# A two-block transformer kernel on one core: token norm folded into the activation before the expert matmuls, GpSimd sums as adding DMAs, gate products on VectorE, a third gelu buffer

## The chip, the cores and the metric

One Trainium2 (trn2) chip, one core. The metric is the device time of one execution in microseconds (us). The kernel before took 2830.65 us in the median of 3 runs (2825.29 to 2832.58).

## The reference, cut to what matters

256 tokens of width 2048 go through two blocks. The change lies in the second half of the first one, a layer of 16384 experts (128 x 128), of which every token uses 128.

```
hn = rms_norm(h, ffn_norm_gain)                      # per token
q = (hn @ w_query).reshape(T, 8, 2, 128)
scores = einsum('thpc,hpnc->thpn', q, sub_keys)
vals, idx = top_k(scores, 16)                        # then the best 16 of 16 x 16 sums
experts, gates = ...                                 # 128 experts and softmax gates per token
u = expert_down[experts]                             # rows of 16384 x 2048
hdn = gelu(einsum('ted,td->te', u, hn))
h = h + einsum('te,ted->td', gates * hdn, expert_up[experts])
```

## The kernel before, in words

Everything is float32. A weight is streamed in units of 128 x 2048 (1 MB) through three raw buffers by SyncE's DMA queue (line 69). Each unit is cut in two halves; of each half ScalarE writes the rounded part `hi` (line 74) and VectorE the rest `lo` (line 75), into five half buffers `whl`. `fm` (lines 100 to 102) then multiplies a unit with the activation `act`, itself a pair hi and lo, by 3 x 16 matmuls of 256 columns: 48 matmuls a unit.

The expert layer (`phase_peer`) computes the dense product for all 16384 experts and picks afterwards:

- **Query**: 16 units of `w_pq`; ScalarE, VectorE and GpSimd find the top 16 (top-k) beside it.
- **Down stage**: 128 units of `expert_down`, in 32 groups of four. Per unit, VectorE multiplies the sums in PSUM with the token's norm factor (`Rb`, line 1007, into `z`), and ScalarE applies gelu into `ghs` (line 968), a buffer of 128 x 4 x 256 for one group; there are two. `act` holds the activation without the norm, since the factor is the same for all features of a token.
- **Place steps**, beside the down stage: 64 steps of four tokens build the dense gate matrix. VectorE makes two one-hot tiles `oe`, `oa` (lines 690, 691); GpSimd (line 698) and ScalarE (line 700) multiply `oe` with the two parts of the gate into `ob`; TensorE places them (line 710, 4 matmuls); ScalarE (717) and VectorE (722) add the parts into `gst`, a buffer for 16 tokens, of which there are two. Every fourth step `used` stores `gst` to `g_d` in HBM from ScalarE's queue (738), and GpSimd adds it to `fsum` (740, 742), which VectorE sums into `F` after 8 of them (744).
- **Before the last place step** the gates are not there yet, so finished gelu groups go to HBM (`gh_d`): they are "late". Afterwards `catch_up`, once per unit, lets GpSimd load a late group into `ght` (892; two buffers), multiply it with the gates `gt` (882; loaded from `g_d`, 877, 1 MB per two groups) and store it to `hm_d` (885). New groups are multiplied in `ghs` (882) and stored from there (885), by the same GpSimd queue.
- **List steps**, beside the catch-up: the list of experts that any token uses (lines 826, 828, 836, 837, matmuls 845).
- **Up stage**: rows of `expert_up` and of `hm_d` are gathered by that list.

The side work is spread over the units by a credit: each unit gives `DV` = 2.6 us (`pump_by`), each step costs what its `step(us, ...)` says, 2.3 for a place step and 2.2 for a list step. Before the fifth unit from the end `drain` runs what is left. Engine queues are in program order.

```
def hidden(j, a, gh, z):
    nc.scalar.activation(gh[:, a, :], z, AF.Gelu_apprx_tanh)
...
    x = pp.tile([128, 4, 256], F32, name="ght", tag="ght%d" % (j % 2))
    nc.gpsimd.dma_start(x.rearrange("p a t -> p (a t)"), gh_d[j])
```

Of the kernel before, what the change touches and what calls it, by code (L numbers as in the profile page):

```python
# [9 lines left out]
F32 = mybir.dt.float32  # L10
# [6 lines left out]
OP = mybir.AluOpType  # L17
# [13 lines left out]
KT = K0 + K1 + KB  # L31
JS = 31
FAR = float(1 << 20)
DV = 2.6
LN2_50 = 34.657359027997264


# [119 lines left out]
def after(k, n, f):  # L157

    k.due.setdefault(k.tick + n, []).append(f)
# [12 lines left out]
def pump_by(k, us):  # L172

    k.credit = min(k.credit + us, 2 * us)
    if not k.bg:
        pump(k)
    while k.bg and k.credit > 0:
        k.credit -= getattr(k.bg[0], "us", 1.5)
        pump(k)


def step(us, f):
    f.us = us
    return f
# [378 lines left out]
def phase_peer(k, A):  # L563
# [5 lines left out]
    with ExitStack() as ctx:  # L569
# [111 lines left out]
        def bc(x):  # L681
            return x[:, :, None].to_broadcast([128, 4, 128])
# [11 lines left out]
        def gates_at(q):  # L694
            ts = slice(4 * q, 4 * q + 4)
            b = pw.tile([128, 4, 2, 128], F32R, name="ob", tag="ob")
            e = hot[q][1]
            nc.gpsimd.tensor_mul(b[:, :, 1, :], e, bc(slot["g"][:, 1, ts].bitcast(F32)))  # L698
            for j in range(4):
                nc.scalar.mul(b[:, j, 0, :], e[:, j, :], slot["g"][:, 0, 4 * q + j:4 * q + j + 1].bitcast(F32))  # L700
            hot[q][1] = b
# [33 lines left out]

        def used(g, x):

            nc.scalar.dma_start(g_d[g], x.rearrange("p i t -> p (i t)"))
            if g % 8 == 0:
                nc.gpsimd.tensor_copy(fsum, x)  # L740
            else:
                nc.gpsimd.tensor_add(fsum, fsum, x)
            if g % 8 == 7:
                nc.vector.tensor_reduce(F[g // 8], fsum, axis=AX.X, op=OP.add)


        L = {}

        def lists_flags():
            stri = pp.tile([128, 128], F32, name="stri")  # L750
            nc.vector.tensor_sub(stri, k.tri, k.ident)
            f = pw.tile([128, 2, 128], F32, name="f01", tag="oh")
            for t in range(2):
                nc.vector.tensor_scalar(f[:, t, :], F[t], 0.0, None, op0=OP.is_gt)
            nc.vector.memset(f[:, :, 4 * JS:4 * JS + 4], 0.0)
            cat = L["cat"] = pw.tile([128, 3, 128], F32, name="cat", tag="oh")
            nc.vector.tensor_mul(cat[:, 2, :], f[:, 0, :], f[:, 1, :])
            for t in range(2):
                nc.vector.tensor_sub(cat[:, t, :], f[:, t, :], cat[:, 2, :])
            L["stri"] = stri  # L760
# [103 lines left out]
        def lists_end():  # L864
            t = pp.tile([128, 2, KT], F32, name="lv")
            nc.scalar.copy(t.rearrange("p e r -> p (e r)"), L["ps"][:, :2 * KT])
            nc.vector.scalar_tensor_tensor(t[:, 0, :], t[:, 1, :], 128.0, t[:, 0, :], op0=OP.mult, op1=OP.add)
            L["idx"] = indices(t[:, 0, :], KT, "l")
            L["ex"] = pp.tile([128, 128], F32, name="lex")
            nc.vector.tensor_scalar(L["ex"], iota, 128.0, pi, op0=OP.mult, op1=OP.add)  # L870


        Gs, late = {}, deque()
# [13 lines left out]
        def load_late(j):  # L887
            if j // 2 not in Gs:
                Gs.clear()
                Gs[j // 2] = load_g(j // 2, "gst%d" % (j // 2 % 2))  # L890
            x = pp.tile([128, 4, 256], F32, name="ght", tag="ght%d" % (j % 2))
            nc.gpsimd.dma_start(x.rearrange("p a t -> p (a t)"), gh_d[j])
            return x, Gs[j // 2]

        def rows(x, hi, lo, t):
            nc.scalar.copy(hi[:, t], x[:, t])
            nc.vector.tensor_sub(lo[:, t], x[:, t], hi[:, t].bitcast(F32))  # L897

        for g in range(16):
            w = st.next()  # L900
            acc = bank(k, "acc")[:, :256]
            if g == 0:
                fm(k, acc, w, k.act, part=(0, 12))
                drain(k)
                fm(k, acc, w, k.act, part=(12, 16))
                z0 = pw.tile([1, 256], F32, name="z0", tag="z", bufs=3)
                nc.gpsimd.memset(z0, 0.0)
                nc.gpsimd.dma_start(hm_d[0:1, :], z0)
            else:
                fm(k, acc, w, k.act)  # L910
            if g == 1:
                ms = k.p_sm.tile([128, 2], F32, name="ms", tag="ms")
                mean_eps(k, ms, k.ss, D)
                rsqrt(k, r, ms)
            if g == 4:
                row_bc(k, Rb, r)
            qT = pw.tile([128, 256], F32, name="qT", tag="qT")
            nc.scalar.copy(qT, acc)
            if g < 2:
                pump(k)  # L920
            else:
                pump_by(k, 3.2)
            k.bg.appendleft(step(0.0, lambda g=g, qT=qT: scores(g, qT)))
            if g % 2:
                k.bg.extend(topk_steps(g // 2))
        state = {}

        def prepare():

            def lag():  # L930
                return step(DV, lambda: None)
            yield step(0.7, last[0])
            for _ in range(3):
                yield step(0.3, lambda: None)
            yield step(2.0, gates)
            yield lag()
            yield step(0.6, to_slots)
            yield lag()
            yield step(1.4, lambda: ones_at(0))
            yield step(1.4, lambda: (ones_at(1), gates_at(0)))  # L940
            for q in range(65):
                yield step(2.3, lambda q=q: place_steps(q))

            def placed():
                state["placed"] = True
            yield step(0.0, placed)
            yield lag()
            yield step(2.0, lists_flags)
            yield lag()
            yield step(0.2, lists_count)  # L950
            yield lag()
            yield step(0.2, lists_sum)
            yield lag()
            yield step(2.5, lists_over)
# [9 lines left out]

        pend = deque()

        def hidden(j, a, gh, z):
            nc.scalar.activation(gh[:, a, :], z, AF.Gelu_apprx_tanh)
            if a < 3:
                return  # L970
            if "placed" not in state:
                nc.scalar.dma_start(gh_d[j], gh.rearrange("p a t -> p (a t)"))
                late.append(j)
                return
            if state.get("g") != j // 2:
                state["g"], state["gt"] = j // 2, load_g(j // 2, "gtd")
            times(gh, state["gt"], j)
            if j == JS:
                hst = state["hst"] = pp.tile([128, 2, 4, 256], F32R, name="hst", tag="gst%d" % (JS // 2 % 2))
                split(k, hst[:, 0], hst[:, 1], gh)  # L980
            else:
                store(j, gh)
# [16 lines left out]
        for i in range(NE):  # L999
            j, a = ORDER[i // 4], i % 4  # L1000
            w = st.next()
            acc = bank(k, "acc")[:, :256]
            fm(k, acc, w, k.act)
            if a == 0:
                gh = pw.tile([128, 4, 256], F32, name="ghs", tag="ghs")
            z = pw.tile([128, 256], F32, name="z", tag="z", bufs=3)
            nc.vector.tensor_mul(z, acc, Rb)
            if i:
                hidden(*prev)
            prev = (j, a, gh, z)  # L1010
# [35 lines left out]
        def overflow():  # L1046
            d = L["d"]
            nc.vector.tensor_scalar(d, d, -128.0 * KT, None, op0=OP.add)
            turns = nc.values_load(L["nx"][0:1, 1:2], min_val=0, max_val=NE)
            with k.tc.If(turns > 0), k.tc.For_i(0, turns, 1) as _:  # L1050
                ps = bank(k, "bg")
                for c in range(NE):
                    a = pw.tile([128, 128], F32, name="xa", tag="xa")
                    nc.vector.tensor_scalar(a, iota, d[:, c:c + 1], None, op0=OP.is_equal)
                    nc.tensor.matmul(ps[:, :1], a, L["ex"][:, c:c + 1], start=c == 0, stop=c == NE - 1)
# [643 lines left out]
```

## Time and profile before

| | |
|---|---|
| median of 3 runs | 2830.65 us |
| the profiled execution | 2830.46 us, span of its instructions 2828.7 us |
| busy share of the span | TensorE 94%, weight loads 86%, VectorE 67%, ScalarE 50%, GpSimd 30% |
| mean granted TensorE clock | 0.973 of full speed |
| moved by DMA | 580.26 MB, 205 GB/s |

The page gives shares over the whole span. Cut by stage they differ widely, so the rows below are windows. A row of a timeline reads: start us, duration us, engine, line, operation, written tile <- read tiles, shapes, and in brackets the idle time before it with what ended it. A group row ends with busy us, mean ns | idle us before, and what ended it.

### The profile page before, as it was taken

To read this page: it belongs to the slowest core of one execution; us is meant where nothing else is said; L and a number is where in the kernel's file an instruction comes from. 1 tells how busy PE (TensorE), PEld (TensorE's weight loads), DVE (VectorE), ACT (ScalarE), POOL (GpSimd) and SP (SyncE) were. 2 spreads that over 40 slices of the span, in tenths; PEclk is the share of its full clock that TensorE was granted. 3 is DMA by queue.
4 is the path that set the end of the run, shared out by engine and by line. 5 is a ranking of instruction groups with operands and counts; after the bars stand their busy time and mean duration, and the time that the engine had idled before them with its cause. 6 is when DMAs were issued, how large, how long until landed. Compare 5 with 4: busy or idle time off the path is not lost. (4 is left out here: it accounts for less than half of the span.)

```text
span 2828.7 us, 45188 instructions
## 1 busy us (share of the span) xinstructions
PE 2654.1 (94%) x18008; PEld 2423.3 (86%) x18008; DVE 1894.3 (67%) x2736; ACT 1409.3 (50%) x2298; POOL 848.6 (30%) x829
## 2 busy tenths in 40 slices
PE   8999999999988988966599999999999999999998
PEld 8977778999988988966597888887899999999886
DVE  5544556999899899755465666666567766555555
ACT  5344455444655566422244555556564444444453
POOL 0001110222244344344514565554145441000001
PEclk9999999999999999978799999999999999999999
DMA  7534435556655655777766888885543445555553
GB/s 281 170 128 136 160 122 180 178 201 217 216 195 194 215 198 213 286 251 275 234 203 235 296 290 295 288 300 189 206 165 135 150 150 185 192 186 187 185 188 134
DMA packets 92391, 580.26 MB, mean 205 GB/s; under 512 B 11216, under 2 KB 11344, under 8 KB 31120
## 3 DMA queue, kind: packets, MB, share of 16 engines
q1 hardware_dynamic: 53696, 381.05, 38.6%
q0 software_dynamic: 31712, 165.63, 16.8%
q10 hardware_dynamic: 6768, 30.65, 2.7%
q8 instruction: 143, 2.34, 0.3%
q14 instruction: 72, 0.59, 0.1%
HBM read 531.14 MB, written 46.14 MB: 204 GB/s over the span
## 5 line engine op out<-in xcount | busy, mean ns | idle before, releaser
L75 DVE TENSOR_TENSOR whl<-raw,whl 128x1024 fp32r<-128x1024 f32 (+2 forms) x917 | 1206.8, 1330 | 661.3 <-ACT whl L74 641.9
L74 ACT CAST whl<-raw 128x1024 fp32r<-128x1024 f32 (+2 forms) x917 | 952.0, 1047 | 717.0 <-PE acc L102 365.4
L100 PE MATMUL acc<-act,whl 128*128 128x256 f32 x3840 | 1086.6, 283 | 0.2
L101 PE MATMUL acc<-act,whl 128*128 128x256 f32 x3840 | 1086.2, 283 | 0.4
L102 PE MATMUL acc<-act,whl 128*128 128x256 f32 x3840 | 1083.8, 282 | 0.0
L102 PEld LDWEIGHTS acc<-act,whl 128*128 128x128 f32 x3840 | 738.2, 192 | 0.0
L100 PEld LDWEIGHTS acc<-act,whl 128*128 128x128 f32 x3840 | 734.1, 191 | 2.3 <-issue 1.2
L101 PEld LDWEIGHTS acc<-act,whl 128*128 128x128 f32 x3840 | 734.4, 191 | 1.0 <-DVE act L217 1.0
L1103 PE MATMUL acc<-whl,hh 128*128 128x512 f32 x864 | 218.2, 396 | 0.0
L1103 PE MATMUL bg<-whl,hh 128*128 128x512 f32 x864 | 217.9, 396 | 0.0
L118 PE MATMUL acc<-whl,act 128*128 128x512 f32 (+1 forms) x512 | 197.6, 386 | 7.8 <-ACT whl L74 6.9
L119 PE MATMUL acc<-whl,act 128*128 128x512 f32 (+1 forms) x512 | 195.2, 381 | 4.4 <-DVE whl L75 4.2
L1103 PEld LDWEIGHTS bg<-whl,hh 128*128 128x128 f32 x864 | 162.2, 188 | 39.5
L1103 PEld LDWEIGHTS acc<-whl,hh 128*128 128x128 f32 x864 | 162.2, 188 | 39.5
L120 PE MATMUL acc<-whl,act 128*128 128x512 f32 (+1 forms) x512 | 195.1, 381 | 0.8 <-DVE act L217 0.8
L1035 POOL DMA_INDIRECT raw<-in_up,idx_l x100 | 133.7, 1337 | 141.3 <-DVE hh L897 77.9
L698 POOL TENSOR_TENSOR ob<-oe,sl_g 128x512 fp32r<-128x512 f32 x64 | 96.0, 1508 | 124.6 <-DVE oe L690 119.9
L118 PEld LDWEIGHTS acc<-whl,act 128*128 128x128 f32 x512 | 96.8, 189 | 29.9 <-ACT whl L74 7.3
L119 PEld LDWEIGHTS acc<-whl,act 128*128 128x128 f32 x512 | 96.7, 189 | 24.8 <-DVE whl L75 6.2
L120 PEld LDWEIGHTS acc<-whl,act 128*128 128x128 f32 x512 | 96.7, 189 | 20.4 <-DVE act L217 1.0
L700 ACT ACTIVATE ob<-oe,sl_g 128x128 fp32r<-128x128 f32 x256 | 81.6, 390 | 63.3 <-DVE gst L722 45.0
L1035 POOL DMA_INDIRECT hr<-hm_d,idx_l x100 | 102.6, 1026 | 32.3 <-issue 32.3
(403 smaller groups left out, 3152.5 us busy)
## 6 DMA issues: line engine op xcount, KB each, us to landing
raw<-in_down SPq DMA_DIRECT2D x128, 1024.0 KB, 5.0
raw<-in_w_cv SPq DMA_DIRECT2D x32, 1024.0 KB, 4.9
raw<-in_w_gg SPq DMA_DIRECT2D x32, 1024.0 KB, 4.9
raw<-in_w_dil SPq DMA_DIRECT2D x24, 1024.0 KB, 4.9
gt<-g_d POOLq DMA_DIRECT2D x17, 1024.0 KB
raw<-in_w_out SPq DMA_DIRECT2D x16, 1024.0 KB, 4.8
raw<-in_w_pq SPq DMA_DIRECT2D x16, 1024.0 KB, 4.9
g_d<-gst ACTq DMA_DIRECT2D x16, 1024.0 KB, 6.7
```

Source lines behind the costliest of these rows:

```text
L74: nc.scalar.copy(hi[:, s], r[:, s])
L75: nc.vector.tensor_sub(lo[:, s], r[:, s], hi[:, s].bitcast(F32))
L100: k.nc.tensor.matmul(acc, hi[:, f], x, start=j == 0, stop=False)
L101: k.nc.tensor.matmul(acc, hi[:, f], y, start=False, stop=False)
L102: k.nc.tensor.matmul(acc, lo[:, f], x, start=False, stop=j == nk - 1)
L118: k.nc.tensor.matmul(accs[t], ah[:, kk, ts], hi[:, m], start=st, stop=False)
L119: k.nc.tensor.matmul(accs[t], ah[:, kk, ts], lo[:, m], start=False, stop=False)
L120: k.nc.tensor.matmul(accs[t], al[:, kk, ts], hi[:, m], start=False, stop=sp)
L698: nc.gpsimd.tensor_mul(b[:, :, 1, :], e, bc(slot["g"][:, 1, ts].bitcast(F32)))
L700: nc.scalar.mul(b[:, j, 0, :], e[:, j, :], slot["g"][:, 0, 4 * q + j:4 * q + j + 1].bitcast(F32))
L1035: nc.gpsimd.indirect_dma_start(out=out, out_offset=None, in_=table, in_offset=bass.IndirectOffsetOnAxis(ap=idx, axis=0), bounds_check=n - ...
L1103: nc.tensor.matmul(accs[2 * s + c][t], x[:, ts], y[:, c * 512:(c + 1) * 512], start=i == 0 and x is hh and y is hi, stop=last_ and i == N - 1)
```

## The change

- `fm` of the last query unit is cut in four parts; behind each part ScalarE and VectorE write a quarter of `act` anew, as the pair hi and lo of the activation times the norm factor. GpSimd has prepared the four products `xr` (128 x 1024, one add and one multiply each) after query units 6, 8, 10 and 12.
- The 128 multiplications by `Rb` in the down stage go; gelu reads PSUM.
- GpSimd's gate product (line 698) goes to VectorE.
- `g_d` is stored from GpSimd's queue. The sums into `fsum` become DMAs on that queue, the first of 8 a copy and the others adding. The sum into `F` is issued three steps later.
- `ghs` and `ght` get a third buffer each. Some small tiles share buffers.
- `DV` becomes 2.9, a place step costs 2.9; one more unit lies between the last place step and the lists.

```diff
-DV = 2.6
+DV = 2.9
...
-            nc.gpsimd.tensor_mul(b[:, :, 1, :], e, bc(slot["g"][:, 1, ts].bitcast(F32)))
+            nc.vector.tensor_mul(b[:, :, 1, :], e, bc(slot["g"][:, 1, ts].bitcast(F32)))
...
-            nc.scalar.dma_start(g_d[g], x.rearrange("p i t -> p (i t)"))
+            nc.gpsimd.dma_start(g_d[g], x.rearrange("p i t -> p (i t)"))
             if g % 8 == 0:
-                nc.gpsimd.tensor_copy(fsum, x)
+                nc.gpsimd.dma_start(fsum, x)
             else:
-                nc.gpsimd.tensor_add(fsum, fsum, x)
+                nc.gpsimd.dma_start(fsum, x, accum_op=OP.add)
             if g % 8 == 7:
-                nc.vector.tensor_reduce(F[g // 8], fsum, axis=AX.X, op=OP.add)
+                after(k, 3, lambda: nc.vector.tensor_reduce(F[g // 8], fsum, axis=AX.X, op=OP.add))
...
-            x = pp.tile([128, 4, 256], F32, name="ght", tag="ght%d" % (j % 2))
+            x = pp.tile([128, 4, 256], F32, name="ght", tag="ght%d" % (j % 3))
...
+            if g == 15:
+                for q in range(4):
+                    fm(k, acc, w, k.act, part=(4 * q, 4 * q + 4))
+                    qs = slice(4 * q, 4 * q + 4)
+                    split(k, k.act[0][:, qs, :], k.act[1][:, qs, :], scaled.pop(0))
...
+            if 6 <= g <= 12 and g % 2 == 0:
+                q = g // 2 - 3
+                x = pw.tile([128, 4, 256], F32, name="xr", tag="ob" if q == 3 else "ghs", bufs=2 if q == 3 else 3)
+                a, b = [o[:, 4 * q:4 * q + 4, :].bitcast(F32) for o in k.act]
+                nc.gpsimd.tensor_add(x, a, b)
+                nc.gpsimd.tensor_mul(x, x, Rb[:, None, :].to_broadcast([128, 4, 256]))
+                scaled.append(x)
...
-                yield step(2.3, lambda q=q: place_steps(q))
+                yield step(2.9, lambda q=q: place_steps(q))
...
+            yield lag()
+            yield lag()
...
-            nc.scalar.activation(gh[:, a, :], z, AF.Gelu_apprx_tanh)
+            nc.scalar.activation(gh[:, a, :], acc, AF.Gelu_apprx_tanh)
...
-                gh = pw.tile([128, 4, 256], F32, name="ghs", tag="ghs")
-            z = pw.tile([128, 256], F32, name="z", tag="z", bufs=3)
-            nc.vector.tensor_mul(z, acc, Rb)
+                gh = pw.tile([128, 4, 256], F32, name="ghs", tag="ghs", bufs=3)
```

The order of VectorE's instructions in the place steps, before (`whl` is the weight split, `sl_i` the expert numbers):

```order
L75 TENSOR_TENSOR whl<-raw,whl 128x1024 x2
L1007 TENSOR_TENSOR z<-acc,R_p 128x256
L722 TENSOR_TENSOR gst<-gst,bg 128x128x2 x2
L690 TENSOR_TENSOR oe<-cst,sl_i_7320 128x512
L691 TENSOR_TENSOR oa<-cst,sl_i_7315 128x512
L722 TENSOR_TENSOR gst<-gst,bg 128x128x2 x2
L690 TENSOR_TENSOR oe<-cst,sl_i_7320 128x512
L691 TENSOR_TENSOR oa<-cst,sl_i_7315 128x512
L75 TENSOR_TENSOR whl<-raw,whl 128x1024 x2
```

and with the change:

```order
L75 TENSOR_TENSOR whl<-raw,whl 128x1024 x2
L722 TENSOR_TENSOR gst<-gst,bg 128x128x2 x2
L690 TENSOR_TENSOR oe<-cst,sl_i_7110 128x512
L691 TENSOR_TENSOR oa<-cst,sl_i_7105 128x512
L698 TENSOR_TENSOR ob<-oe,sl_g 128x4x128
L75 TENSOR_TENSOR whl<-raw,whl 128x1024 x2
```

The product `z` is gone and the gate product is VectorE's. Before, some units have two place steps (64 steps lie beside 57 units); now every unit has one (64 beside 64). GpSimd's queue in the same steps is now

```order
L738 DMA g_d<-gst 128x2048
L742 DMA fsum<-gst 128x2048
L738 DMA g_d<-gst 128x2048
L742 DMA fsum<-gst 128x2048
L738 DMA g_d<-gst 128x2048
```

and nothing else: the products and the sums that stood there four to one have left it.

In the catch-up, GpSimd's queue was (`ghs` is a new group, `ght` a late one)

```order
L892 DMA ght<-gh_d 128x1024
L877 DMA gt<-g_d 128x16x128
L882 TENSOR_TENSOR ghs<-ghs,gt 128x1024
L885 DMA hm_d<-ghs 128x4x256
L882 TENSOR_TENSOR ght<-ght,gt 128x1024
L885 DMA hm_d<-ght 128x4x256
L892 DMA ght<-gh_d 128x1024
L882 TENSOR_TENSOR ght<-ght,gt 128x1024
L885 DMA hm_d<-ght 128x4x256
```

and is now

```order
L890 DMA ght<-gh_d 128x1024
L875 DMA gt<-g_d 128x16x128
L880 TENSOR_TENSOR ghs<-ghs,gt 128x1024
L883 DMA hm_d<-ghs 128x4x256
L880 TENSOR_TENSOR ght<-ght,gt 128x1024
L883 DMA hm_d<-ght 128x4x256
L875 DMA gt<-g_d 128x16x128
L890 DMA ght<-gh_d 128x1024
L880 TENSOR_TENSOR ght<-ght,gt 128x1024
```

The kinds and their order stay. What moves is that 23 groups are late where 21 were, and the buffer that a load of `ght` waits for was stored one late group earlier. At the end of the lists, in `drain`, VectorE now has five list steps in a row without a weight split between the last three (before, one step was left):

```order
L826 TENSOR_TENSOR oe<-cst,lrp 128x400
L828 TENSOR_TENSOR oa<-cst,lrp 128x512
L837 TENSOR_TENSOR ob<-oe,cst 128x4x100
L826 TENSOR_TENSOR oe<-cst,lrp 128x400
L828 TENSOR_TENSOR oa<-cst,lrp 128x512
L837 TENSOR_TENSOR ob<-oe,cst 128x4x100 x2
```

TensorE has 20 list matmuls (five steps) there in one piece; before, the last step lay behind a unit of its own.

## Rows read from the trace of the kernel before

**Rows 1.** Windows by stage: start:end, length, busy us (count) per engine, PEclk, DMA share, GB/s.

```profile
506.00:561.00 55.00, 55.00 (x475) 55.00 (x474) 51.21 (x140) 26.86 (x45) 14.10 (x17) 1.00 0.50 173
561.00:731.00 170.00, 170.00 (x1461) 170.00 (x1460) 154.60 (x371) 79.65 (x105) 40.46 (x41) 1.00 0.60 208
731.00:1133.00 402.00, 359.43 (x2943) 355.64 (x2941) 372.68 (x419) 243.56 (x546) 163.13 (x78) 0.96 0.58 205
1205.00:1410.00 205.00, 126.42 (x935) 124.79 (x934) 101.84 (x112) 53.57 (x76) 99.33 (x77) 0.78 0.73 251
1410.00:1495.00 85.00, 76.56 (x621) 75.89 (x620) 55.53 (x74) 36.09 (x50) 14.04 (x8) 0.94 0.61 205
1150.00:1170.00 20.00, 20.00 (x175) 20.00 (x174) 12.37 (x20) 9.00 (x12) 1.14 (x1) 1.00 0.99 356
```

**Rows 2.** Waits in the place steps: who <- for whom: us in total, times, longest.

```profile
PE bg L710 <- POOL ob L698: 27.7, 13, 7.1
PE bg L710 <- DVE gst L722: 14.9, 6, 5.7
```

**Rows 3.** Timeline around one sum of GpSimd in the place steps, 909 to 919 us.

```profile
909.25 5.03 POOL L742 TENSOR_TENSOR fsum<-fsum,gst 128x2048 f32<-128x2048 f32 x1 [11.09 <-DVE gst L722]
909.69 5.14 DVE L691 TENSOR_TENSOR oa<-cst,sl_i 128x512 fp32r<-128x512 f32 x1
914.23 3.48 POOL L698 TENSOR_TENSOR ob<-oe,sl_g 128x512 fp32r<-128x512 f32 x2
...
915.78 0.74 PE L710 MATMUL bg<-ob,oa 128*128 128x256 f32 x4 [1.71 <-POOL ob L698]
```

**Rows 4.** Groups by line and form in the place steps, 731 to 1133 us.

```profile
L75 DVE TENSOR_TENSOR whl<-raw,whl 128x1024 fp32r<-128x1024 f32 x112 | 178.0, 1618 | 15.4 <-ACT whl L74 15.3
L691 DVE TENSOR_TENSOR oa<-cst,sl_i 128x512 fp32r<-128x512 f32 x63 | 99.3, 1577 | 0.0
L722 DVE TENSOR_TENSOR gst<-gst,bg 128x256 f32<-128x256 f32 x124 | 45.8, 409 | 0.0
L690 DVE TENSOR_TENSOR oe<-cst,sl_i 128x512 f32<-128x512 f32 x63 | 45.0, 715 | 0.3 <-POOL ob L698 0.3
L1007 DVE TENSOR_TENSOR z<-acc,R_p 128x256 f32<-128x256 f32 x56 | 23.3, 415 | 8.9 <-PE acc L102 8.9
...
L698 POOL TENSOR_TENSOR ob<-oe,sl_g 128x512 fp32r<-128x512 f32 x63 | 94.5, 1509 | 108.4 <-DVE oe L690 103.8 <-PE bg L710 4.0 <-PE acc L102 0.7
L742 POOL TENSOR_TENSOR fsum<-fsum,gst 128x2048 f32<-128x2048 f32 x13 | 64.6, 4971 | 104.0 <-DVE gst L722 104.0
```

**Rows 5.** Groups by line and form in the catch-up, 1205 to 1410 us.

```profile
L882 POOL TENSOR_TENSOR ghs<-ghs,gt 128x1024 f32<-128x1024 f32 x6 | 14.2, 2360 | 31.1 <-DMA gt<-g_d 19.7 <-issue 11.3
L877 POOL DMA_DIRECT2D gt<-g_d x12 | 14.0, 1166 | 0.0
...
L892 POOL DMA_DIRECT2D ght<-gh_d x17 | 9.4, 555 | 67.3 <-DMA hm_d<-ght 67.3
L968 ACT ACTIVATE ghs<-z 128x256 f32<-128x256 f32 x19 | 7.9, 413 | 102.2 <-DMA hm_d<-ghs 101.1 <-DVE z L1007 1.1
```

**Rows 6.** Timeline of GpSimd: first and last of six new groups, five periods apart.

```profile
1171.08 2.40 POOL L882 TENSOR_TENSOR ghs<-ghs,gt 128x1024 f32<-128x1024 f32 x1 [19.93 <-issue]
...
1395.24 2.33 POOL L882 TENSOR_TENSOR ghs<-ghs,gt 128x1024 f32<-128x1024 f32 x1 [8.81 <-DMA gt<-g_d]
```

**Rows 7.** DMA over 1200 to 1400 us: GB/s in 40 slices of 5 us.

```profile
GB/s 358 274 361 101 105 114 375 275 374 321 170 348 329 112 193 350 411 305 171 356 311 7 179 210 306 349 408 316 166 319 166 247 292 195 315 310 300 374 174 53
```

**Rows 8.** DMA issues: queue, count, KB each, median us from issue to landing.

```profile
g_d<-gst ACTq DMA_DIRECT2D x16, 1024.0 KB, 6.7
```

**Rows 9.** Timeline of VectorE, one list step, 1414 us.

```profile
1414.02 0.56 DVE L826 TENSOR_TENSOR oe<-cst,lrp 128x400 f32<-128x400 f32 x1
1414.50 0.68 DVE L828 TENSOR_TENSOR oa<-cst,lrp 128x512 fp32r<-128x512 f32 x1
1415.10 0.56 DVE L837 TENSOR_TENSOR ob<-oe,cst 128x400 fp32r<-128x400 f32 x1
```

More of the change, by code (lines that the diff above doesn't have):

```diff
@@ L736, in used @@
         def used(g, x):
-            nc.scalar.dma_start(g_d[g], x.rearrange("p i t -> p (i t)"))
+            nc.gpsimd.dma_start(g_d[g], x.rearrange("p i t -> p (i t)"))
             if g % 8 == 0:
-                nc.gpsimd.tensor_copy(fsum, x)
+                nc.gpsimd.dma_start(fsum, x)
             else:
-                nc.gpsimd.tensor_add(fsum, fsum, x)
+                nc.gpsimd.dma_start(fsum, x, accum_op=OP.add)
             if g % 8 == 7:
-                nc.vector.tensor_reduce(F[g // 8], fsum, axis=AX.X, op=OP.add)
+                after(k, 3, lambda: nc.vector.tensor_reduce(F[g // 8], fsum, axis=AX.X, op=OP.add))
         L = {}
         def lists_flags():
-            stri = pp.tile([128, 128], F32, name="stri")
+            stri = pw.tile([128, 128], F32, name="stri", tag="tk")
             nc.vector.tensor_sub(stri, k.tri, k.ident)
@@ L868, in lists_end @@
             L["idx"] = indices(t[:, 0, :], KT, "l")
-            L["ex"] = pp.tile([128, 128], F32, name="lex")
-            nc.vector.tensor_scalar(L["ex"], iota, 128.0, pi, op0=OP.mult, op1=OP.add)
         Gs, late = {}, deque()
@@ L897, in rows @@
             nc.vector.tensor_sub(lo[:, t], x[:, t], hi[:, t].bitcast(F32))
+        scaled = []
         for g in range(16):
@@ L901, in phase_peer @@
             acc = bank(k, "acc")[:, :256]
-            if g == 0:
+            if g == 15:
[3 more added lines that the diff above has]
+                    split(k, k.act[0][:, qs, :], k.act[1][:, qs, :], scaled.pop(0))
+            elif g == 0:
                 fm(k, acc, w, k.act, part=(0, 12))
@@ L905, in phase_peer @@
                 fm(k, acc, w, k.act, part=(12, 16))
-                z0 = pw.tile([1, 256], F32, name="z0", tag="z", bufs=3)
+                z0 = pw.tile([1, 256], F32, name="z0", tag="qT")
                 nc.gpsimd.memset(z0, 0.0)
@@ L965, in phase_peer, with hidden @@
         pend = deque()
-        def hidden(j, a, gh, z):
-            nc.scalar.activation(gh[:, a, :], z, AF.Gelu_apprx_tanh)
+        def hidden(j, a, gh, acc):
+            nc.scalar.activation(gh[:, a, :], acc, AF.Gelu_apprx_tanh)
             if a < 3:
@@ L1004, in phase_peer @@
             if a == 0:
-                gh = pw.tile([128, 4, 256], F32, name="ghs", tag="ghs")
-            z = pw.tile([128, 256], F32, name="z", tag="z", bufs=3)
-            nc.vector.tensor_mul(z, acc, Rb)
+                gh = pw.tile([128, 4, 256], F32, name="ghs", tag="ghs", bufs=3)
             if i:
                 hidden(*prev)
-            prev = (j, a, gh, z)
+            prev = (j, a, gh, acc)
             if i == NE - 1:
@@ L1048, in overflow @@
             nc.vector.tensor_scalar(d, d, -128.0 * KT, None, op0=OP.add)
+            ex = pw.tile([128, 128], F32, name="xe", tag="xe", bufs=1)
+            nc.vector.tensor_scalar(ex, iota, 128.0, pi, op0=OP.mult, op1=OP.add)
             turns = nc.values_load(L["nx"][0:1, 1:2], min_val=0, max_val=NE)
@@ L1054, in overflow @@
                     nc.vector.tensor_scalar(a, iota, d[:, c:c + 1], None, op0=OP.is_equal)
-                    nc.tensor.matmul(ps[:, :1], a, L["ex"][:, c:c + 1], start=c == 0, stop=c == NE - 1)
+                    nc.tensor.matmul(ps[:, :1], a, ex[:, c:c + 1], start=c == 0, stop=c == NE - 1)
                 v = pp.tile([128, 1], F32, name="xv")
```

## The prediction

> **What bounds the kernel now.** I read the windows by stage first, since TensorE's 94% over the whole span hides where it falls behind. A pace is wanted for that. From 561 to 731 us TensorE is busy in every microsecond and runs 1461 matmuls in 170 us, 8.594 per us [rows 1]. A down unit of 48 matmuls with one place or list step of 4 is then 52 / 8.594 = 6.05 us, and four units are 24.2 us. Against this pace each later stage has a loss: its length less its matmuls over 8.594. The place steps (731 to 1133 us) lose 402 - 2943 / 8.594 = 59.6 us, the catch-up (1205 to 1410 us) 205 - 935 / 8.594 = 96.2 us, and the stretch to the up stage 85 - 621 / 8.594 = 12.7 us [rows 1]. These 168 us are all that the change can win, for elsewhere TensorE is full. The granted clock (0.96 and 0.78 of 2.4 GHz) is in these counts already.
>
> Next come the waits and the timeline of the place steps, for who ends the waits. TensorE waits 27.7 us for GpSimd's `ob` and 14.9 us for VectorE's `gst` [rows 2]; the rest is lower clock behind the gaps. The timeline shows the cause: while GpSimd's sum runs for 5.03 us, VectorE's `oa` beside it takes 5.14 us, and GpSimd's gate products come only after the sum, so that TensorE waits [rows 3]. The groups say it over the stage: `oa` means 1577 ns where `oe`, of the same size, means 715 [rows 4]. VectorE's 372.68 busy us of 402 [rows 1] are therefore largely time in which it is held.
>
> In the catch-up the groups show one long wait: ScalarE's gelu stands 101.1 us for the store of `ghs` to `hm_d` [rows 5]. That store is late because GpSimd's queue is: its loads of `ght` stand 67.3 us for the store of the buffer they overwrite, and the product of a new group stands 31.1 us for its gates [rows 5]. From the first to the last of six new groups pass 1395.24 - 1171.08 = 224.2 us [rows 6], 44.8 us per period of four units where TensorE's pace wants 24.2. Five times the excess of 20.6 us is 103 us, which is the gelu's wait. So the catch-up is bound by GpSimd's chain of transfers.
>
> **The change, part by part.**
>
> Place steps. The sums (13 x 4971 ns) and gate products (63 x 1509 ns) [rows 4] leave GpSimd, which has only DMAs to issue there. VectorE loses `z` (415 ns a unit) and gets the product, which I take like `oe` at 715 ns at most. Its step is then two weight splits, two `gst` sums of 409, and three tiles of up to 715. A split means 1618 ns held [rows 4]; with nothing beside it I bound it by twice the 512-column tile, 1.43 us. That is 2.86 + 0.82 + 2.15 = 5.8 us at most, under 6.05. ScalarE's 243.56 us of 402 [rows 1] leave it room to read PSUM in the gelu. So TensorE becomes the bound, and I take 4 us of the 59.6 as left: **-56 us** (ends -30 and -60; the upper end leaves half, as VectorE has only 0.2 us of room by the bound). One place step per unit instead of 1.13 makes no work; it moves two more groups to the late ones, counted in the catch-up.
>
> Adding DMAs. No row shows one. The nearest transfers of 1 MB: the store of `gst` lands after 6.7 us [rows 8], and GpSimd once stood 19.93 us for gates [rows 6]. `gst` has two buffers, so store and sum together have four units, 24.2 us, before ScalarE overwrites the buffer. The sum is issued behind the store on the same queue. With 6.7 + 6.7 us it is hidden; with 6.7 + 19.9 = 26.6 us, each of 14 later buffers waits 2.4 us, 34 us. I take the store's value, the same bytes in the same long rows, at nothing. The bytes fit too: at 0.58 busy share [rows 1] the stage has room. GpSimd's queue waits for the earlier sum before the next, with nothing but the next store behind it. The sum into `F` now waits on VectorE for a landing; twice, up to a unit late: **+3 us** (0 to 6).
>
> Catch-up. The third `ght` lets a load overwrite a buffer stored one late group earlier, so the 67.3 us go: over 205 / 44.8 = 4.6 periods, 14.7 us each, which leaves 30.1 us a period if nothing takes their place. What is late next is the DMA. A period moves four late groups in and out (8 x 0.52 MB), 2.5 loads of gates (12 in 4.6 periods [rows 5], 1.05 MB each), one new group out (0.52) and four weight units (4.2): 11.5 MB. At the 356 GB/s of the stretch with 0.99 DMA share [rows 1] that is 32.4 us. The waits for gates, 31.1 / 4.6 = 6.8 us a period [rows 5], are times in which GpSimd's queue issues nothing, and they stay: 39.2 us. The third `ghs` lets the gelu run one group further ahead, worth one group's 24.2 us once. The two late groups more, with their gates, are 2 x 1.57 MB, 9 us at 356 GB/s. Loss: 5 x (39.2 - 24.2) - 24.2 + 9 = 60 us, where 101 were: **-41 us**. Ends: a period of 30.1 us leaves 14 (-87); of 44.8 leaves 88 (-13). I take 39.2 since the DMA share in the catch-up is already 0.73 while TensorE runs at 935 / (205 x 8.594) = 53% of its pace [rows 1]. The rate carries this term. The Trainium skill, "DMA: Bandwidth & Descriptors", section "Where 436 GB/s comes from", puts the ceiling at 435 GB/s; by that the period would be 33.2 us and the sum 30 us lower. The stretch at 0.99 share measures 356, so the row decides.
>
> Query. GpSimd gets 8 operations on 1024 columns, 2.4 us each by `ghs` [rows 5], 19 us, in a stretch where VectorE is busy 51.21 of 55 us [rows 1]. Rows 3 show VectorE held by such an operation. If all 19 us hold it, less 4 us of room, TensorE loses 16; if they fall on top-k's work or are covered by half buffers made ahead, nothing. VectorE's weight splits fill under half of its time there, so **+4 us** (0 to 16). The Trainium skill, "SBUF — State Buffer", section "Who interferes with whom", says that of a VectorE operation with two SBUF inputs and a GpSimd one that reads SBUF the later is blocked to the other's end, which speaks against this part: by it alone the cost is the upper end, and the time 12 us later. Rows 3 agree for a tile with two such inputs; much of the top-k work has one.
>
> The four rewrites of `act` follow their quarter of the last query unit (12 matmuls, 1.4 us each); the first down unit reads the last quarter three quarters, 4.2 us, after its first. They cost nothing; without that cover it is a few us, once.
>
> End. `drain` has four more list steps of VectorE at 0.56 + 0.68 + 0.56 = 1.8 us [rows 9], which TensorE waits for in a row: **+7 us** (0 to 10).
>
> Sum against the profiled execution's 2830.46 us (0.2 us below the median of the runs): -56 - 41 + 3 + 4 + 7 = -83, so **2747 us**.
>
> **The rivals.**
>
> *GpSimd's chain stays.* The waits for `ght` turn into waits for the loads themselves, which the queue now issues with less time before their use; the period stays 44.8 us. For it: loads, gates and stores share one queue. Against it: two loads are under way. Only the third `ghs` gains in the catch-up, 13 us for 41: 2747 + 28 = 2775 us.
>
> *The DMA gives more.* Single slices of the catch-up reach 411 GB/s [rows 7]. If this rate holds whenever there is work, a period is 28.0 + 6.8 = 34.8 us, the loss 5 x 10.6 - 24.2 + 9 = 38 us, and the time 2747 - 22 = 2725 us. The page's ceiling named above points the same way.
>
> *GpSimd's eight operations hold VectorE for all of their 19 us.* As the query part works out, the upper end of 16 us comes: 2747 + 12 = 2759 us. Against it is the top-k work, which lies between the splits.
>
> *VectorE becomes the bound of the place steps.* If its step with the gate product takes 6.9 us, the 56 us are lost again: 2803 us. Against it are the 5.8 us above, all upper bounds.
>
> *The adding DMA is slow* (the other side). If reading, adding and writing back takes 30 us, store and sum take 36.7, 12.5 over the 24.2 that the two `gst` buffers allow; ScalarE stands at line 717 in 14 groups, TensorE behind it: 14 x 12.5 = 175, 2747 + 175 = 2922 us. It decides from 83 / 14 = 5.9 us over, a sum of 23.4 us, which is 3.5 times the store. No row excludes it; the store and the long rows speak against it.
>
> **How the numbers follow.** Forecast 0.43, held for all of the 19 us 0.10, chain stays 0.20, more DMA 0.13, VectorE 0.05, slow adding DMA 0.09. Slower by over 0.3% (8.5 us, about what a measurement of this kernel can tell from no change) is the last less its mild part: 0.08. Within 0.3%: 0.02, a slow sum just at its point. Faster: 0.90. The range: down to 2695, the catch-up's best end (46 us lower) and 6 us of costs that don't come; up to 2805, which holds the chain that stays, VectorE, and an adding DMA of 19.9 us (+34) with one more bad end.
>
> **What would show it.** In the profile after: place steps with 8.5 or more matmuls per us and `oa` and `oe` both near 0.7 us; no wait of line 717 for a DMA; `z` gone. In the catch-up, loads of `ght` that hardly wait for stores, new groups 37 to 41 us apart, the gelu's wait for `hm_d` near 60 us. In the query, weight splits beside `xr` of over 2 us and hardly a gap on TensorE. The prediction is wrong in its main step if the gelu's wait stays near 100 us or goes to nothing, and in its sign if ScalarE stands for the sums into `fsum`.

## The result, and the profile after

The changed kernel takes 2751.0 us in the median of 4 runs (2749.1 to 2755.6), before 2828.5 us beside it: a ratio of 0.973 (95% interval 0.971 to 0.975), 77 us faster. The forecast was 2747. The profiled execution's span is 2753.8 us, 74.9 less than before's.

By the same measure as before (length less matmuls over 8.594 per us), the windows by stage of the changed kernel (columns: window, length, busy us and instructions of PE, PEld, DVE, ACT, POOL, then granted clock, DMA share, GB/s):

```profile
560.00:570.00 10.00, 3.97 (x34) 3.77 (x33) 8.92 (x31) 6.16 (x9) 4.95 (x5) 0.87 0.44 139
570.00:580.00 10.00, 7.29 (x43) 7.30 (x44) 9.93 (x16) 1.05 (x1) 1.51 (x3) 0.62 0.45 168
731.00:1117.00 386.00, 386.00 (x3293) 386.00 (x3293) 306.55 (x442) 260.14 (x569) 21.14 (x30) 1.00 0.82 276
1117.00:1180.00 63.00, 63.00 (x543) 63.00 (x542) 38.67 (x55) 26.58 (x35) 14.01 (x14) 1.00 0.93 326
1180.00:1380.00 200.00, 163.31 (x1254) 161.28 (x1253) 168.38 (x147) 72.39 (x104) 115.23 (x87) 0.90 0.88 309
1380.00:1420.00 40.00, 20.31 (x142) 19.64 (x141) 9.19 (x10) 9.08 (x12) 11.03 (x8) 0.75 0.50 171
```

| stage | loss before | loss after | forecast | measured |
|---|---|---|---|---|
| end of the query | 0 | 20 - 77 / 8.594 = 11.0 | +4 | +11 |
| place steps | 59.6 | 386 - 3293 / 8.594 = 2.8 | -56 | -57 |
| sums into `F` | in the above | 0 (1117 to 1180 us is full) | +3 | 0 |
| catch-up | 96.2 | 200 - 1254 / 8.594 = 54.1 | -41 | -42 |
| to the up stage | 12.7 | 40 - 142 / 8.594 = 23.5 | +7 | +11 |

The measured column adds up to -77, the span fell by 74.9. So each stage went the way that was said, but three of the five rows (query, catch-up, the way to the up stage) hide another cause than the forecast's, as the traces and the experiments show.

**Place steps.** The groups by line of the changed kernel, VectorE, 731 to 1117 us (busy us, mean ns | idle us before, what ended it):

```profile
L75 DVE TENSOR_TENSOR whl<-raw,whl 128x1024 fp32r<-128x1024 f32 x128 | 156.6, 1224 | 79.5 <-ACT whl L74 79.5
...
L691 DVE TENSOR_TENSOR oa<-cst,sl_i 128x512 fp32r<-128x512 f32 x62 | 42.6, 687 | 0.0
```

Splits and `oa` are short now; before they were 1618 and 1577 ns [rows 4]. A step takes 306.55 / 64 = 4.8 us of VectorE, under the 5.8 that were bounded, and no wait of line 717 for a DMA appears. The DMA issues of the changed kernel, 800 to 1000 us (count, size, median us from issue to landing):

```profile
g_d<-gst POOLq DMA_DIRECT2D x8, 1024.0 KB, 7.9
fsum<-gst POOLq DMA_DIRECT2D x8, 1024.0 KB, 15.5
```

The sum lands after 15.5 us (a median of eight issues, one of them a copy) where the forecast took the store's 6.7 [rows 8]; store and sum overlap, and 24.2 us cover both.

**Catch-up.** VectorE's groups (by line), 1180 to 1380 us:

```profile
L75 DVE TENSOR_TENSOR whl<-raw,whl 128x1024 fp32r<-128x1024 f32 x47 | 84.4, 1818 | 29.1 <-ACT whl L74 29.0
L826 DVE TENSOR_TENSOR oe<-cst,lrp 128x400 f32<-128x400 f32 x32 | 33.5, 1046 | 0.8
L828 DVE TENSOR_TENSOR oa<-cst,lrp 128x512 fp32r<-128x512 f32 x32 | 31.7, 990 | 0.0
L837 DVE TENSOR_TENSOR ob<-oe,cst 128x400 fp32r<-128x400 f32 x32 | 26.5, 831 | 0.0
```

And the waits of the same stretch (engine, line, waited for: us, times, longest):

```profile
POOL ght L880 <- DMA ght<-gh_d: 40.2, 9, 7.6
PE bg L845 <- DVE ob L837: 36.7, 12, 7.4
```

The gelu's 101.1 us for the store of `ghs` [rows 5] are gone altogether; about 60 had been forecast. TensorE now stands for VectorE's list tiles (and its weight loads 24.9 us for ScalarE's, which wait for VectorE), and GpSimd for loads of late groups. Yet the groups in GpSimd's queue are as far apart as was said. Its timeline, a load of gates, then the first, fifth and sixth new group:

```profile
1157.68 1.17 POOL L875 DMA_DIRECT2D gt<-g_d  x1
1179.59 2.40 POOL L880 TENSOR_TENSOR ghs<-ghs,gt 128x1024 f32<-128x1024 f32 x1 [20.75 <-issue]
...
1325.27 2.42 POOL L880 TENSOR_TENSOR ghs<-ghs,gt 128x1024 f32<-128x1024 f32 x1
1375.31 2.38 POOL L880 TENSOR_TENSOR ghs<-ghs,gt 128x1024 f32<-128x1024 f32 x1 [6.66 <-DMA gt<-g_d]
```

and ScalarE's, the last gelu of the first and of the sixth of these groups:

```profile
1149.47 0.38 ACT L982 ACTIVATE ghs<-acc 128x256 f32<-128x256 f32 x1
...
1302.04 0.37 ACT L982 ACTIVATE ghs<-acc 128x256 f32<-128x256 f32 x1
```

On GpSimd, five periods take 195.7 us, 39.1 us each, where 39.2 was the forecast. (Long and short periods alternate, and five hold three long ones; over four, to the fifth group, it is 36.4 us here and 43.4 in the kernel before.) GpSimd does not wait for the gelu: the product of a group starts 30 to 73 us after the group's last gelu. Where it stands before a new group, it stands for the gates: those loaded at 1157.68 us landed 21.8 us later, and the product followed at 1179.59; before the second, fourth and sixth group it is the same, with landings after 13.8, 16.3 and 7.7 us. TensorE, though, runs ahead of this queue, with three `ghs` buffers to do it in: its groups are (1302.04 - 1149.47) / 5 = 30.5 us apart, and not 39. So the forecast's period is there, but TensorE does not keep to it, and something else keeps TensorE from its 24.2. That is the first thing to test.

**The two new losses.** At the end of the query, GpSimd's `xr` operations (groups, 505 to 565 us), VectorE's timeline, and TensorE's wait:

```profile
L932 POOL TENSOR_TENSOR xr<-act,act 128x1024 f32<-128x1024 f32 x4 | 13.5, 3384 | 0.0
L933 POOL TENSOR_TENSOR xr<-xr,R_p 128x1024 f32<-128x1024 f32 x4 | 13.1, 3273 | 0.3
```

```profile
571.44 3.48 DVE L214 TENSOR_TENSOR act<-xr,act 128x1024 fp32r<-128x1024 f32 x3
```

```profile
PE acc L101 <- DVE act L214: 8.7, 1, 8.7
```

The operations take 3.3 us, not 2.4. VectorE's queue is behind by then: the rewriting, cast by ScalarE from 559 us on, is reached at 571.4. Before the up stage, waits of 1375 to 1435 us:

```profile
ACT hst L213 <- POOL ghs L880: 16.3, 1, 16.3
...
POOL ghs L880 <- DMA gt<-g_d: 15.1, 2, 8.4
...
PE bg L1117 <- DVEq L1064: 13.3, 1, 13.3
...
DVE xe L1062 <- DMA hm_d<-ghs: 7.6, 1, 7.6
```

ScalarE stands with the split of the last-but-one group (`hst`) behind GpSimd's product of it, which waits for its gates; and the branch of line 1064 is late, because `xe`, computed ahead of it in memory that the last `ghs` held, waits for the last store. Neither is a list step, which the forecast named for this stage: the last list matmuls run at 1371 us, so that `drain` falls into the catch-up's row, where TensorE stands 5.6 us for list tiles between 1355 and 1380 us.

### The profile page after: what moved, and what is told of

Its sections match the earlier page's. It is cut to its first block, busy times and chain, and to the rows that moved or that the text cites. A ratio compares the mean times of both kernels' runs of the same rounds, so it can differ in the third digit from the quotient of the medians.

```text
span 2753.8 us, 44962 instructions
## 1 busy us (share of the span) xinstructions
PE 2644.3 (96%) x18008; PEld 2416.5 (88%) x18008; DVE 1831.7 (67%) x2676; ACT 1411.2 (51%) x2302; POOL 727.9 (26%) x791
## 5 line engine op out<-in xcount | busy, mean ns | idle before, releaser
L75 DVE TENSOR_TENSOR whl<-raw,whl 128x1024 fp32r<-128x1024 f32 (+2 forms) x917 | 1188.7, 1306 | 646.1 <-ACT whl L74 634.1
L738 POOL DMA_DIRECT2D g_d<-gst x16 | 8.9, 556 | 395.7 <-DVE gst L722 395.7
```

What stands on the lines that cost most here:

```text
L75: nc.vector.tensor_sub(lo[:, s], r[:, s], hi[:, s].bitcast(F32))
```

## The experiments

Theory A is the forecast's: the chain of GpSimd's transfers sets TensorE's pace in the catch-up. Theory B: VectorE sets it, held by GpSimd's products. Differences are of medians; medians of before beside the runs lie between 2828.5 and 2831.0 us.

**Two `ght` buffers.**

```
-tag="ght%d" % (j % 3)
+tag="ght%d" % (j % 2)
```

> The changed kernel with two ght buffers instead of three, nothing else. Theory A (my forecast): the catch-up is bound by GpSimd's chain of transfers, so its loads stand again some 60 us for stores of ght, the period between new groups goes from 39 to about 45 us, and the time rises by about 34 us. Theory B (from the trace after): the catch-up is bound by VectorE, which GpSimd's products hold; waits on GpSimd's queue come back but the products are as many as before, TensorE's waits for the list tiles stay what ends last, and the time rises by 0 to 10 us.

Measured: 2787.0 us (2783.6 to 2790.0), 0.985 of before (0.983 to 0.987), +36 over the changed kernel. Waits, 1180 to 1380 us:

```profile
POOL ght L890 <- DMA hm_d<-ght: 79.1, 17, 11.6
...
ACT ghs L982 <- DMA hm_d<-ghs: 56.7, 4, 19.7
```

A is right here: loads wait for stores, new groups are 46.2 us apart (1181.1 to 1412.3 us, five periods), the gelu stands for stores again.

**Two `ghs` buffers** (`bufs=3` to `bufs=2`).

> The changed kernel with two ghs buffers instead of three (the scaled parts of the activation lie in two ghs and two ob buffers). Theory A (my forecast): one group's run ahead is lost once and the gelu waits again for stores of ghs, +24 us. Theory B: the gelu never waits for a store in the changed kernel, since the loads of ght no longer hold up the queue, so the third ghs buffer is worth 0 to 5 us.

Measured: 2763.8 us (2763.3 to 2766.0), 0.978 (0.976 to 0.979), +13. Groups 38.8 us apart over five periods, as in the changed kernel. Waits, 1180 to 1380 us:

```profile
ACT ghs L982 <- DMA hm_d<-ghs: 62.9, 6, 18.4
```

Between the two expectations. With two buffers the gelu stands 62.9 us for stores, as A says; with three it stands for none, and yet the time is only 13 us shorter. So the chain alone does not explain the changed kernel.

**No products.** GpSimd's multiplication by the gates is left out for all groups but one, which leaves loads, gates and stores as they are.

```
-nc.gpsimd.tensor_mul(x, x, gt[:, (j % 2) * 4:(j % 2) * 4 + 4])
+if j == JS:
+    nc.gpsimd.tensor_mul(x, x, gt[:, (j % 2) * 4:(j % 2) * 4 + 4])
```

> The changed kernel without GpSimd's products of the gelu groups with the gates (all but the last group's); loads, gates and stores stay. The output is another. If VectorE, held by the products, binds the catch-up, its splits and list tiles run at their short durations and most of the 54 us lost between 1180 and 1380 us come back: -35 to -50 us. If the transfers bind it (39 us per four units), the groups stay about 37 us apart and the loss stays within 10 us.

Measured: 2715.1 us (2714.7 to 2716.8), 0.960 (0.958 to 0.961), -36. A window, then VectorE's groups (1180 to 1380 us):

```profile
1180.00:1320.00 140.00, 134.66 (x1145) 133.80 (x1144) 96.42 (x129) 65.59 (x93) 35.64 (x46) 1.00 1.01 374
```

```profile
L75 DVE TENSOR_TENSOR whl<-raw,whl 128x1024 fp32r<-128x1024 f32 x53 | 64.5, 1224 | 53.4 <-ACT whl L74 47.1 <-DVEq L1065 6.0
L828 DVE TENSOR_TENSOR oa<-cst,lrp 128x512 fp32r<-128x512 f32 x32 | 21.9, 686 | 0.0
L826 DVE TENSOR_TENSOR oe<-cst,lrp 128x400 f32<-128x400 f32 x32 | 18.3, 571 | 0.8
L837 DVE TENSOR_TENSOR ob<-oe,cst 128x400 fp32r<-128x400 f32 x32 | 18.1, 570 | 0.0
```

B, for TensorE. In these 140 us the loss is 140 - 1145 / 8.594 = 6.8 us; in the changed kernel 140 - 895 / 8.594 = 35.9. A's distance between the groups is still there: stores of new groups are 36.2 us apart over five periods, 35.9 over four. Three `ghs` buffers carry the gelu over that for these few groups; it stands only 5.8 us for stores. Behind 1320 us, up to the first matmul of the up stage, most of the loss stays: 60 - 238 / 8.594 = 32.3 us, in the changed kernel 100 - 502 / 8.594 = 41.6. So the hold accounts for the 29 us before 1320 us, and for little behind. The held time: in the changed kernel a split is longer by 594 ns, the list tiles by 475, 304 and 261, together 47 x 0.594 + 32 x 1.040 = 61 us, beside 28 products of 2.5 us.

**Norm per unit, with two `ghs` buffers**: `z` back on VectorE, no `xr`, no rewriting.

```
+z = pw.tile([128, 256], F32, name="z", tag="z", bufs=3)
+nc.vector.tensor_mul(z, acc, Rb)
-prev = (j, a, gh, acc)
+prev = (j, a, gh, z)
```

> Against the run with two ghs buffers (2763.8 us): the norm factor back as one product z per unit on VectorE, no xr, no rewriting of the activation. The stall of about 11 us at the end of the query goes. If the transfers bind the catch-up (as the gelu's 62.9 us wait for stores in that run says), z costs nothing there: 2753 us. If VectorE binds it, z costs 0.415 us in each of some 24 units: 2763 us.

Measured: 2753.0 us (2752.3 to 2755.0), 0.973 (0.972 to 0.975), 11 faster than the run with two `ghs` buffers, as A says for a kernel whose gelu waits for stores. The end of the query is full (560 to 580 us: 174 matmuls). So folding the norm costs its 11 us and wins none by itself: the place steps are full with `z` too (386 of 386 us). Its worth is the memory of `z`: with `z` and three `ghs` buffers the pool would take 44.5 KB of each partition, where 41.5 are left. The third buffer wins 13 us and the folding costs 11, so that the two edits together are worth 2 us, which is within the spread of the runs.

**Sums on GpSimd** and **gate products on GpSimd**, one at a time.

```
-nc.gpsimd.dma_start(fsum, x, accum_op=OP.add)
+nc.gpsimd.tensor_add(fsum, fsum, x)
```

> The changed kernel with the sums into fsum back on GpSimd as copy and additions, the gate products still on VectorE. Fourteen sums of 5 us hold VectorE; it has 79 us of idle time in the place steps. If that idle time takes the holds up, +0 to +8 us. If every sum stalls TensorE as it did before (about 2 us each in waits for gst, and the clock behind it), +25 to +35 us. If the adding DMAs themselves slow other transfers in the changed kernel (DMA busy share 0.82 in these steps), a gain shows.

```
-nc.vector.tensor_mul(b[:, :, 1, :], e, bc(slot["g"][:, 1, ts].bitcast(F32)))
+nc.gpsimd.tensor_mul(b[:, :, 1, :], e, bc(slot["g"][:, 1, ts].bitcast(F32)))
```

> The changed kernel with the gate products back on GpSimd, the adding DMAs kept. The products (63 of 1.5 us beside VectorE) no longer stand behind a sum on GpSimd's queue. If before's loss in the place steps came from the two together, this alone costs 0 to 5 us there. If the products alone hold VectorE enough (1.5 us a unit of its 1.24 us of idle time), TensorE falls behind in the place steps again: +10 to +20 us. The sums alone on GpSimd cost 16.9 us over the changed kernel, 14 of them in the place steps.

Measured: sums on GpSimd 2767.9 us (2766.3 to 2769.1), 0.979 (0.977 to 0.980), +17; gate products on GpSimd 2752.9 us (2751.6 to 2757.7), 0.973 (0.971 to 0.975), no difference. Window and VectorE's groups, 731 to 1117 us, first with the sums, then with the gate products on GpSimd:

```profile
731.00:1117.00 386.00, 374.20 (x3171) 372.13 (x3170) 356.34 (x425) 251.71 (x549) 71.34 (x30) 1.00 0.65 225
```

```profile
L75 DVE TENSOR_TENSOR whl<-raw,whl 128x1024 fp32r<-128x1024 f32 x122 | 147.7, 1227 | 29.7 <-ACT whl L74 29.6
L691 DVE TENSOR_TENSOR oa<-cst,sl_i 128x512 fp32r<-128x512 f32 x61 | 107.1, 1756 | 0.0
```

```profile
731.00:1117.00 386.00, 386.00 (x3293) 386.00 (x3293) 319.11 (x379) 259.79 (x568) 96.35 (x92) 1.00 0.83 276
```

```profile
L75 DVE TENSOR_TENSOR whl<-raw,whl 128x1024 fp32r<-128x1024 f32 x128 | 203.5, 1600 | 66.4 <-ACT whl L74 66.3
```

The loss is 386 - 3171 / 8.594 = 17.0 us with the sums (between the two expectations), 2.8 with the gate products, which lengthen the splits but fit into VectorE's idle time. So once the sums are DMAs, moving the products is worth nothing. In the kernel before, with both on GpSimd, it was 59.6. Where the other 43 us came from is not shown: from the pair, products queued behind a sum [rows 3], or from what else differs there, `z`, the store on ScalarE's queue and 64 place steps beside 57 units instead of 64. The changed kernel with both on GpSimd was not run; the run with faster place steps, below, bears on the last of these.

**Every sum twice.**

```
 nc.gpsimd.dma_start(fsum, x, accum_op=OP.add)
+nc.gpsimd.dma_start(fsum, x, accum_op=OP.add)
```

> The changed kernel with every adding DMA into fsum issued twice in a row (F doubles, which leaves its flags as they are). In the changed kernel an adding DMA lands 15.5 us after its issue (median) and nobody waits. The second one waits for the first. If both land in 31 us or more, ScalarE stands 7 us or more for each of 14 gst buffers: +100 us or more, which would show how near the adding DMA lies to its bound. If the second takes no longer than the plain store (7.9 us), both fit in the 24.2 us that two buffers allow: +0 to +10 us.

Measured: 2785.4 us (2782.1 to 2787.8), 0.985 (0.983 to 0.986), +34. Waits, 731 to 1130 us:

```profile
POOL fsum L743 <- DMA fsum<-gst: 148.6, 12, 14.9
...
ACT gst L717 <- DMA fsum<-gst: 37.2, 8, 6.9
```

Between the two expectations. The second sum waits 148.6 / 12 = 12.4 us for the first to land; together they overrun the 24.2 us for 8 buffers, by up to 6.9 us. The place steps lose 386 - 3165 / 8.594 = 17.7 us (731 to 1117 us), and 63 - 427 / 8.594 = 13.3 go behind them (1117 to 1180 us), where VectorE's second sum into `F` waits 18.7 us. So one adding DMA fits and two do not: the forecast's margin was real, but less than it said.

**Query and end.** Top-k gets less credit late in the query; `xe` is made inside the branch.

```
-pump_by(k, 3.2)
+pump_by(k, 3.2 if g < 6 else 2.0)
...
 with k.tc.If(turns > 0), k.tc.For_i(0, turns, 1) as _:
     ps = bank(k, "bg")
+    ex = pw.tile([128, 128], F32, name="xe", tag="xe", bufs=1)
+    nc.vector.tensor_scalar(ex, iota, 128.0, pi, op0=OP.mult, op1=OP.add)
```

> The changed kernel with two edits in different stages. Query: the credit of the top-k steps falls from 3.2 to 2.0 us per unit from the seventh unit on, so that VectorE is not behind when the activation is rewritten; if the stall of TensorE between 560 and 580 us comes from VectorE's queue, it falls from some 11 us to 0 to 3, and the place steps begin two to four units later, which the catch-up gives back in part (0 to 6 us). End: xe is made inside the branch that is not taken; if the branch was late because xe waits 7.6 us for the last store of ghs, the first matmuls of the up stage come 8 to 12 us earlier; if the gathers set the start anyway, nothing. Together -10 to -22 us if both causes hold, -8 if one does, 0 if none.

Measured: 2741.6 us (2741.4 to 2743.2), 0.969 (0.968 to 0.971), -9. The query's window, and a wait between 1370 and 1425 us:

```profile
560.00:580.00 20.00, 19.53 (x164) 19.16 (x164) 19.72 (x44) 12.41 (x17) 4.52 (x6) 1.00 0.51 184
```

```profile
ACT hst L213 <- POOL ghs L880: 29.5, 1, 29.5
```

Close to the -8 that was expected if one of the two causes holds. The query's stall falls from 11.0 to 20 - 164 / 8.594 = 0.9 us, so its cause was what stood in VectorE's queue ahead of the rewriting. The branch no longer waits 13 us, but what it gave went into a longer wait of ScalarE for `hst`.

**Split late**, on top: the split into `hst` is issued after the last unit.

```
-split(k, hst[:, 0], hst[:, 1], gh)
+state["split"] = lambda: split(k, hst[:, 0], hst[:, 1], gh)
...
     hidden(*prev)
+    state["split"]()
```

> The kernel of the run with the two edits at the query and the end (2741.6 us), and the split of the last-but-one group's product into hst is issued after the last unit instead of right behind its gelu. In that run ScalarE stands 29.5 us for this group's product, and TensorE runs 17 matmuls between 1380 and 1400 us. If the stall comes from that place on ScalarE's queue, TensorE has no gap there: -10 to -16 us. If the late chain of transfers sets the end anyway (the last groups' products wait for their gates), 0 to -4 us.

Measured: 2737.5 us (2733.8 to 2738.9), 0.967 (0.965 to 0.969), -4. ScalarE's wait for this product falls from 29.5 to 6.7 us, but the last-but-one product still waits 11.1 us for its gates, and TensorE stands 12.2 us at the branch, behind which the split now lies.

**Gates early**, on top.

```
 store(j, gh)
+if j % 2 and j < JS - 1:
+    state["g"], state["gt"] = j // 2 + 1, load_g(j // 2 + 1, "gtd")
```

> The kernel of the run before it in this call, and the gates of the next pair of new groups are loaded right behind the store of the pair before, so that GpSimd's products of new groups no longer wait for gates (23.3 us in the run with two edits). If GpSimd's chain of transfers binds the catch-up, its waits fall by these 23 us and the time by 10 to 20 us. If VectorE, held by the products, binds it, 0 to -4 us.

Measured: 2731.6 us (2726.7 to 2734.7), 0.965 (0.962 to 0.967), -6; the ranges of the two runs touch, so the step is small if it is one. Between 1370 and 1425 us GpSimd's products no longer wait for gates, but 27.2 us for the gelu instead: there TensorE is the later one, which is what B expects.

**Place steps faster**, on top: `step(2.9` to `step(2.5`.

> The kernel of the run before it in this call, and a place step costs 2.5 us of credit instead of 2.9, 1.16 steps a unit. VectorE has 79 us of idle time in the place steps of the changed kernel. The gates are ready some 8 units earlier, two groups fewer are late, and the rest is spread over more units. If the catch-up is short of VectorE or of transfers, -10 to -20 us. If the place steps fall behind again by a sum or store that lands too late (20.9 us for a pair of buffers instead of 24.2), the gain is given back there: 0 or slower.

Measured: 2738.2 us (2734.6 to 2741.7), 0.967 (0.965 to 0.969), +7; again the ranges touch. The window of the place steps:

```profile
731.00:1117.00 386.00, 370.63 (x3120) 369.04 (x3119) 301.00 (x441) 255.27 (x565) 24.37 (x34) 0.99 0.82 267
```

In the place steps TensorE now stands for the tiles `ob` (17.0 us for ScalarE's, 10.2 for VectorE's), and line 717 for no DMA: slower, but not for the reason given. The loss there is 386 - 3120 / 8.594 = 23.0 us where it was 2.8, with nothing but DMAs on GpSimd; the stages behind give back some 13 of it. So 1.16 place steps a unit cost TensorE some 20 us by themselves. The kernel before had 64 steps beside 57 units, 1.12, and the change to one a unit is therefore one more candidate for the part of the 59.6 us that the sums do not explain.

**Products on VectorE**, on top of the gates early.

```
-nc.gpsimd.tensor_mul(x, x, gt[:, (j % 2) * 4:(j % 2) * 4 + 4])
+nc.vector.tensor_mul(x, x, gt[:, (j % 2) * 4:(j % 2) * 4 + 4])
```

> The kernel of the run with the gates loaded early (2731.6 us), and all products of gelu groups with gates are made by VectorE instead of GpSimd. Without the products at all, the splits and list tiles of the catch-up run at their short durations (1.22 us a split instead of 1.82) and TensorE keeps its pace up to 1320 us. If it is GpSimd's products that hold VectorE, 28 products of 1.22 us on VectorE itself cost half of the 61 us by which they lengthened its instructions: -10 to -25 us. Against it: VectorE now stands itself for loads of ght where GpSimd stood 46 us for them, and its splits stand behind: if these stands weigh more, +5 to +30 us.

Measured: 2759.5 us (2759.4 to 2761.3), 0.975 (0.974 to 0.977), +28. VectorE's groups, 1180 to 1380 us:

```profile
L75 DVE TENSOR_TENSOR whl<-raw,whl 128x1024 fp32r<-128x1024 f32 x46 | 54.7, 1220 | 12.9 <-ACT whl L74 12.9
L880 DVE TENSOR_TENSOR ght<-ght,gt 128x1024 f32<-128x1024 f32 x22 | 26.9, 1222 | 55.3 <-issue 32.7 <-DMA ght<-gh_d 22.6
```

Both halves of the expectation hold: a product takes 1.2 us and nothing else is lengthened (the list tiles mean 570, 685 and 569 ns), which shows that the products on GpSimd did that. But VectorE now stands 55 us in front of the products of late groups, with the splits behind it.

## Why the prediction was right, and where it was not

- **Place steps, -56 (measured -57).** Right in size, and in VectorE's part (4.8 us a step, 5.8 at most had been said). The forecast did not part the edits. Measured one at a time, the sums are worth 17 us, the products nothing once the sums are moved, and one step a unit instead of 1.16 some 20; how the rest divides is open.
- **Adding DMAs, 0 (measured 0).** Right, but the sum was sized by the store's 6.7 us and lands after 15.5. One behind the other, as the forecast reckoned, store and sum would take 7.9 + 15.5 = 23.4 of the 24.2 us; that they overlap left more room than that, though not enough for two sums.
- **Sums into `F`, +3 (0).** VectorE waited once for 6.4 us; ready half buffers covered it.
- **Catch-up, -41 (-42).** The step that failed is the loss as five times the excess of the chain's period ("5 x (39.2 - 24.2) - 24.2 + 9"), and with it "the rate carries this term". The third `ght` did what was said: without it 46.2 us a period and +36. The chain's period came nearly as said, too: 39.1 us, with waits for gates of (12.76 + 15.28 + 6.66) / 5 = 6.9 us where 6.8 were said. But with three `ghs` buffers TensorE does not follow it: no gelu waits for a store, and TensorE's groups are 30.5 us apart. Up to 1320 us what holds TensorE is VectorE, held by GpSimd's products: without them TensorE is near its pace while the stores stay 36.2 us apart, and 374 GB/s flow, not the 356 of the nearest row [rows 1]. The forecast used that hold in the place steps and the query, and left it out of the catch-up, whose products it knew. So it is luck that the term fits to 1 us. The sign that the prediction gave for an error in its main step, a gelu's wait that goes to nothing, did appear.
- **Query, +4 (+11).** The size came near the rival of operations that hold VectorE for all their time (upper end 16; 19 less 4 is 15), but not by its path. An operation took 3.3 us beside VectorE, not 2.4, and the splits beside it meant 1865 ns where they had meant 1380; TensorE did not stand for splits, though, but 8.7 us for the rewritten activation. So "they cost nothing", of the four rewrites, failed: they stood in VectorE's queue behind top-k and the held splits, and with less top-k there the stall goes while the operations stay.
- **End, +7 (+11).** The list steps were not it: `hst` on ScalarE's queue and `xe` ahead of the branch were. `xe` stands in the diff; that its memory is free only after the last store was not looked up.

The misses are of either sign (-1, -3, -1, +7, +4), so the sum is 6 us from the measured -77. Part of that is luck: in three of the five terms the cause was another than the one forecast.

## What to carry to other kernels

A forecast period that is met is no proof of its cause: take away the suspected hold (here: no products) and see whether the pace returns. Where GpSimd works on SBUF beside VectorE, as its products do here, charge its time to VectorE in every stage, and look whether VectorE has the idle time to take it up: in the place steps the products fitted, in the catch-up they did not. Two queues that hand buffers to each other can have different periods while the buffers last: measure both before one is said to bind the other. A rewritten operand or a temporary that is "off the path" stands in a queue: look at what is in front of it, and at who last held its memory.

The edits at the query, the end and the gates together make the fastest complete version here: 2731.6 us, 19 below the changed kernel. What stays open is a way to relieve VectorE in the catch-up without letting it stand for loads.

## What the runs showed of the hardware

- Which instructions the hold strikes: in the run with gate products on GpSimd VectorE's split, with two inputs in SBUF, grows from 1224 to 1600 ns in the mean, in the run with sums there `oa` from 687 to 1756. Line 722, one of whose inputs is in PSUM, hardly ever meets a GpSimd instruction; in the kernel before it did at 948.89 us, beside a gate product (948.51 us, 1.36 long), and two of it took 0.74 us as elsewhere. The Trainium skill, "SBUF — State Buffer", section "Who interferes with whom", says that a VectorE instruction with two SBUF inputs contends with a GpSimd instruction that reads SBUF, and that one with at most one such input, outside VectorE's 2-port modes, does not; the rows agree.
- GpSimd seems to be slower too: `xr` operations of 1024 columns took 3.3 us beside a busy VectorE, products of as many columns before the up stage (1392 us), beside an idle one, 2.3 us. Their operands differ, and no run tried the same operation both ways.
- An adding DMA of 1 MB landed 15.5 us after its issue (the median) beside a store of the same bytes at 7.9; a second sum behind it waited 12.4 us on average for the first to land.
